# Row sums of 16384 rows: the last store in two halves on two queues, three blocks of rows instead of two, another cut of the last row

## The chip, the cores and the metric

The kernel runs on one core of a Trainium2 chip. The metric is the time of one execution on the device in microseconds (us), as the median of several runs; lower is better. The profile is of one execution, with its times counted from the span's start. SyncE (SP) and ScalarE (ACT) can each issue DMAs; VectorE (DVE) and ScalarE compute here, TensorE and GpSimd do no work of the kernel.

## The reference

```python
x = np.random.randn(32, 512, 1024).astype(np.float32)
return np.sum(x, axis=-1).astype(np.float32)
```

It is 32 x 512 = 16384 rows of 1024 floats (4 KB each), 67.11 MB in all, and one sum for each row: 64 KB of output.

## The kernel before

The 128 partitions take 128 rows each. The rows lie in two blocks. In the first, partition p owns 113 consecutive rows of the input (`BODY`), so neighbouring partitions are 113 x 4 KB = 452 KB apart. In the second, it owns 15 (`LAST`), 60 KB apart. A row sum goes to one column of a result tile: `res_a` with 113 columns, `res_z` with 15. Each tile is stored as one contiguous stretch of the output, 452 B and 60 B a partition.

Loads are all issued by SyncE, in the order of the list `loads` (L86 to L95, issued at L130 to L133): one row into `lead` (the first sum can begin early), then seven groups of 16 rows into the three buffers `xt` in turn, then the last block in pieces. `CUTS = (0, 8, 12, 14)` gives pieces of 8, 4 and 2 rows in one more `xt` buffer; the last row goes into `tail` in two parts, cut at column `CUT = 656`, so 656 and 368 columns. From the fourth group on a load waits until VectorE has finished the group that held its buffer (`freed`, L132). The first two loads are moved into the program's entry (L166 to L175), ahead of the engines' first meeting.

VectorE reduces rows with `tensor_reduce` (`rows_dve`, L58): the lead row, six groups of 16 rows, 9 rows of the seventh. ScalarE takes the other 7 of that group with an activation that accumulates (`rows_act`, L69). Of each of the first two pieces VectorE takes half the rows and ScalarE half, 4 and 4, then 2 and 2. Of the third piece ScalarE takes one row, and VectorE one by `pairs_dve` (L76): it adds the two halves of the row elementwise while it accumulates the sum, so 1024 columns are 512 pairs. The last row is made of two such sums:

```python
pairs_dve(tail, 0, CUT, tail[:, CUT + 14 : CUT + 15], pairs[0])
nc.vector.wait_ge(sems["tail1"], 16)
nc.vector.wait_ge(vec, count["vec"])
pairs_dve(tail, CUT + 14, D + 16, res_z[:, 14:15], pairs[1])
```

The first sums 328 pairs and puts its result beside the columns of the second part, with a zero, so the second sums 185 pairs: the 368 columns, the first result and the zero. VectorE therefore waits at L126 for its own previous result.

SyncE stores twice. The early store of `res_a` (L137) waits for the first part of the last row to land (L134) and for the sums of the groups; the last store of `res_z` (L140) waits for all counts of VectorE (`vec`) and ScalarE (`act`). At the end SyncE waits for the early store, clears the semaphores (L144), and waits for the last store (L145).

Of the kernel before, what the change touches and what calls it, by code (L numbers as in the profile page):

```python
# [6 lines left out]
COPY = mybir.ActivationFunctionType.Copy  # L7
X = mybir.AxisListType.X

LEAD = 1  # L10
G = 16
BODY = LEAD + 7 * G
LAST = 15
BUFS = 3
ACT_ROWS = 7
CUT = 656
CUTS = (0, 8, 12, 14)
EARLY = 2


def row_sums(nc, x: bass.AP, out: bass.AP):
    P = nc.NUM_PARTITIONS
    x_flat = x.flatten_outer_dims()
    R, D = x_flat.shape
    C = R // P
    assert R % P == 0 and C == BODY + LAST
    out_flat = out.rearrange("a (b c) -> (a b c)", c=1)

    def block(r0, n):
        x_b = x_flat[r0 : r0 + P * n].rearrange("(p c) d -> p (c d)", p=P)  # L30
        out_b = out_flat[r0 : r0 + P * n].rearrange("(p c) -> p c", p=P)
        return x_b, out_b

    x_a, out_a = block(0, BODY)
    x_z, out_z = block(P * BODY, LAST)

    def sbuf(name, n):
        return nc.alloc_sbuf_tensor(name, [P, n], F32)

    xt = [sbuf(f"xt{i}", G * D) for i in range(BUFS)]  # L40
    lead = sbuf("lead", LEAD * D)
    tail = sbuf("tail", D + 16)
    pairs = [sbuf(f"pairs{i}", D // 2) for i in range(3)]
    res_a = sbuf("res_a", BODY)
    res_z = sbuf("res_z", LAST)

    names = [f"slot{i}" for i in range(BUFS)] + ["first", "piece0", "piece1", "piece2", "tail0"]
    names += ["tail1", "vec", "act", "early_store", "store"]
    sems = {n: nc.alloc_semaphore(n) for n in names}
    slots = [sems[f"slot{i}"] for i in range(BUFS)]  # L50
    vec, act = sems["vec"], sems["act"]
    numbers = [s.num for s in sems.values()]
    assert numbers == list(range(numbers[0], numbers[0] + len(numbers)))

    count = {"vec": 0, "act": 0}

    def rows_dve(t, j, n, res, c):
        nc.vector.tensor_reduce(  # L58
            out=res[:, c : c + n],
            in_=t[:, j * D : (j + n) * D].rearrange("p (j d) -> p j d", d=D),  # L60
            axis=X,
            op=ADD,
        ).then_inc(vec, 1)
        count["vec"] += 1

    def rows_act(t, j, n, res, c):
        for i in range(n):
            v = t[:, (j + i) * D : (j + i + 1) * D]
            nc.scalar.activation(  # L69
                out=v, in_=v, func=COPY, accum_out=res[:, c + i : c + i + 1]  # L70
            ).then_inc(act, 1)
            count["act"] += 1

    def pairs_dve(t, a, b, acc, pairs):
        h = (a + b) // 2
        nc.vector.tensor_tensor_reduce(  # L76
            out=pairs[:, 0 : h - a], in0=t[:, a:h], in1=t[:, h:b], scale=1.0, scalar=0.0,
            op0=ADD, op1=ADD, accum_out=acc,
        ).then_inc(vec, 1)
        count["vec"] += 1  # L80

    n_bufs = (BODY - LEAD) // G


    freed = {}
    loads = [(0, lead[:, :], x_a[:, 0 : LEAD * D], sems["first"])]  # L86
    for b in range(n_bufs):
        c = LEAD + b * G
        loads.append((b, xt[b % BUFS][:, :], x_a[:, c * D : (c + G) * D], slots[b % BUFS]))
    last = xt[n_bufs % BUFS]  # L90
    for k, (i, j) in enumerate(zip(CUTS, CUTS[1:])):
        loads.append((n_bufs, last[:, i * D : j * D], x_z[:, i * D : j * D], sems[f"piece{k}"]))
    for k, (i, j, gap) in enumerate(((0, CUT, 0), (CUT, D, 16))):
        e = (LAST - 1) * D
        loads.append((0, tail[:, i + gap : j + gap], x_z[:, e + i : e + j], sems[f"tail{k}"]))  # L95


    nc.vector.memset(tail[:, CUT + 15 : CUT + 16], 0.0).then_inc(vec, 1)  # L98
    count["vec"] += 1
    nc.vector.wait_ge(sems["first"], 16)  # L100
    rows_dve(lead, 0, LEAD, res_a, 0)
    for b in range(n_bufs):
        a = ACT_ROWS if b == n_bufs - 1 else 0
        nc.vector.wait_ge(slots[b % BUFS], 16 * (b // BUFS + 1))
        rows_dve(xt[b % BUFS], 0, G - a, res_a, LEAD + b * G)
        freed[b] = count["vec"]
        if a:
            nc.scalar.wait_ge(slots[b % BUFS], 16 * (b // BUFS + 1))
            rows_act(xt[b % BUFS], G - a, a, res_a, LEAD + b * G + G - a)
    body_vec, body_act = count["vec"], count["act"]  # L110

    for k in range(2):
        i, j = CUTS[k], CUTS[k + 1]
        h = (j - i) // 2
        nc.vector.wait_ge(sems[f"piece{k}"], 16)
        rows_dve(last, i, h, res_z, i)
        nc.scalar.wait_ge(sems[f"piece{k}"], 16)
        rows_act(last, i + h, j - i - h, res_z, i + h)
    nc.scalar.wait_ge(sems["piece2"], 16)
    rows_act(last, 13, 1, res_z, 13)  # L120
    nc.vector.wait_ge(sems["piece2"], 16)
    pairs_dve(last, 12 * D, 13 * D, res_z[:, 12:13], pairs[2])
    nc.vector.wait_ge(sems["tail0"], 16)
    pairs_dve(tail, 0, CUT, tail[:, CUT + 14 : CUT + 15], pairs[0])
    nc.vector.wait_ge(sems["tail1"], 16)
    nc.vector.wait_ge(vec, count["vec"])  # L126
    pairs_dve(tail, CUT + 14, D + 16, res_z[:, 14:15], pairs[1])


    for b, dst, src, s in loads:  # L130
        if b >= BUFS:
            nc.sync.wait_ge(vec, freed[b - BUFS])  # L132
        nc.sync.dma_start(out=dst, in_=src).then_inc(s, 16)  # L133
    nc.sync.wait_ge(sems["tail0"], 16)  # L134
    nc.sync.wait_ge(vec, body_vec)
    nc.sync.wait_ge(act, body_act)
    nc.sync.dma_start(out=out_a, in_=res_a[:, :]).then_inc(sems["early_store"], 16)  # L137
    nc.sync.wait_ge(vec, count["vec"])
    nc.sync.wait_ge(act, count["act"])
    nc.sync.dma_start(out=out_z, in_=res_z[:, :]).then_inc(sems["store"], 16)  # L140


    nc.sync.wait_ge(sems["early_store"], 16)
    nc.sync.sem_clear(range(numbers[0], sems["store"].num))  # L144
    nc.sync.wait_ge(sems["store"], 16).then_inc(sems["store"], -16)  # L145


def kernel(tc: tile.TileContext, x: bass.AP, out: bass.AP):
    tc.close()
    tc.compile()  # L150
    nc = tc.nc
    row_sums(nc, x, out)

    sp = mybir.EngineType.SP
    fn = nc.m.functions[0]
    entry, body = None, None
    for blk in fn.blocks:
        ops = [i for i in blk.instructions if i.engine == sp]  # L160
        if entry is None:
            entry = blk
        elif any(i.opcode == "DMACopy" for i in ops):
            body = blk
            break
    code = list(body.instructions)  # L166
    loads = [i for i in code if i.engine == sp and i.opcode == "DMACopy"][:EARLY]
    for load in loads:
        assert not load.sync_info.on_wait
        code.remove(load)  # L170
    body.instructions = code
    code = list(entry.instructions)
    at = next(k for k, i in enumerate(code) if i.engine == sp and i.opcode == "Drain")
    code[at:at] = loads
    entry.instructions = code  # L175
# [29 lines left out]
```

## Time and profile before

| what | value |
|---|---|
| median of 3 runs | 160.99 us (160.79 to 161.18) |
| span of the profiled execution | 159.7 us |
| outside the span, against the median | 1.3 us |
| VectorE busy | 122.6 us (77%) |
| ScalarE busy | 16.3 us (10%) |
| DMA packets | 2160, all on SyncE's queue, 97.8% of the 16 engines' span |

The profile gives the profiled execution's span and no other time of its own; what lies around the span is taken as the difference to the median. Packets are counted with the small ones that report a landing. A stretch of the trace ("windows") gives the busy time of each engine in it, the granted clock, the mean busy share of the 16 DMA engines and GB/s. Short stretches can show a share above 1.00 and uneven GB/s, because a packet is put down to the time at which it is listed.

In the chain of waits, "DMA" stands for the time until a load landed, "SPq" for SyncE issuing a DMA, "DVEq" for VectorE's sequencer. A pair sum shows as two instructions, the sum itself and a read of the accumulator (0.08 us) that overlaps its end.

### The profile page before, as it was taken

Reading aid. Unit: us, or ns where it says so; the run is one execution under the profiler, and the core shown is the slowest. Engines: PE = TensorE matmul, PEld = TensorE weight load, DVE = VectorE, ACT = ScalarE, POOL = GpSimd, SP = SyncE. Lnnn points to the kernel's source line nnn. Section 1 sums busy time; section 2 is a strip of 40 time slices with the busy share of each in tenths; the row PEclk is TensorE's granted clock in tenths of the full one; section 3 lists DMA queues with packets and bytes.
Section 4 is the critical chain, followed back from the end, with each engine's and each line's share of the span. In section 5 each row is a group of like instructions: output and inputs, shape, how many; then the busy total and the mean of one; then the engine's idle time right before and its main releaser. Section 6 shows DMA issues by size and latency. Waiting matters only on the chain.

```text
span 159.7 us, 105 instructions
## 1 busy us (share of the span) xinstructions
DVE 122.6 (77%) x17; ACT 16.3 (10%) x29; POOL 0.2 (0%) x4
## 2 busy tenths in 40 slices
DVE  1100029999499985999779996899949999499984
ACT  3000000000000000000000000000000000196783
POOL 0000000000000000000000000000000000000000
DMA  9969969979799699699699699699796996999993
GB/s 394 525 263 525 509 279 525 460 328 525 328 460 525 263 525 525 263 525 525 263 525 509 279 525 492 295 525 443 345 525 295 492 525 295 476 410 394 435 394 107
DMA packets 2160, 67.18 MB, mean 421 GB/s; under 512 B 496, under 2 KB 624, under 8 KB 880
## 3 DMA queue, kind: packets, MB, share of 16 engines
q1 hardware_dynamic: 2160, 67.18, 97.8%
HBM read 67.11 MB, written 0.07 MB: 421 GB/s over the span
## 4 chain that ended last, share of the span: by engine, by line
DMA 75%; DVE 22%; SPq 1%; issue 0%; DVEq 0%
DMA xt<-in_x_dram 51%; DMA tail<-in_x_dram 24%; DVE res_a L58 22%; SPq L133 1%; DVE pairs L76 1%; DVEq L126 0%; DVE tail L76 0%; DVE res_z L76 0%
## 5 line engine op out<-in xcount | busy, mean ns | idle before, releaser
L58 DVE TENSOR_REDUCE res_a<-xt 128x16 f32<-128x16384 f32 (+1 forms) x7 | 113.1, 16155 | 31.0 <-DMA xt<-in_x_dram 31.0
L69 ACT ACTIVATE xt<-xt 128x1024 f32<-128x1024 f32 x14 | 14.6, 1045 | 139.1 <-DMA xt<-in_x_dram 139.1
L58 DVE TENSOR_REDUCE res_z<-xt 128x4 f32<-128x4096 f32 (+1 forms) x2 | 6.7, 3352 | 0.5 <-DMA xt<-in_x_dram 0.5
L69 ACT ACTIVATION_READ_ACCUMULATOR xt<-xt 128x1 f32 x14 | 2.6, 187 | 0.0
L58 DVE TENSOR_REDUCE res_a<-lead 128x1 f32<-128x1024 f32 x1 | 1.2, 1219 | 1.4 <-DMA lead<-in_x_dram 1.4
L98 DVE MEMSET tail<- 128x1 f32 x1 | 0.1, 59 | 2.0 <-PEq L150 2.0
L69 ACT ACT_TABLE_LOAD x1 | 1.3, 1283 | 1.9 <-PEq L150 1.9
L76 DVE CUSTOM_DVE_ANT_0 pairs<-tail 128x328 f32<-128x328 f32 (+1 forms) x2 | 0.9, 427 | 0.3
L76 DVE CUSTOM_DVE_ANT_0 pairs<-xt 128x512 f32<-128x512 f32 x1 | 0.7, 693 | 0.2 <-DMA xt<-in_x_dram 0.2
L76 DVE DVE_READ_ACCUMULATOR2_ANT res_z<- 128x1 f32 x2 | 0.2, 83 | 0.0
L189 POOL MEMSET const-uint8-127<- 128x1 uint8 x1 | 0.1, 102 | 0.0
L189 POOL MEMSET const-bfloat16-1.0<- 128x1 bf16 x1 | 0.1, 101 | 0.0
L189 POOL MEMSET const-float32-0.0<- 128x1 f32 x1 | 0.1, 98 | 0.2 <-issue 0.2
L189 POOL MEMSET const-float32-1.0<- 128x1 f32 x1 | 0.1, 98 | 0.0
L76 DVE DVE_READ_ACCUMULATOR2_ANT tail<- 128x1 f32 x1 | 0.1, 82 | 0.0
## 6 DMA issues: line engine op xcount, KB each, us to landing
xt<-in_x_dram SPq DMA_DIRECT2D x1, 4096.0 KB, 31.2
xt<-in_x_dram SPq DMA_DIRECT2D x1, 2048.0 KB, 35.7
xt<-in_x_dram SPq DMA_DIRECT2D x1, 1024.0 KB, 37.7
lead<-in_x_dram SPq DMA_DIRECT2D x1, 512.0 KB, 3.4
tail<-in_x_dram SPq DMA_DIRECT2D x1, 328.0 KB, 38.0
tail<-in_x_dram SPq DMA_DIRECT2D x1, 184.0 KB, 37.9
xt<-in_x_dram SPq DMA_DIRECT2D x7, 40.8
out_dram<-res_a SPq DMA_DIRECT2D x1, 56.5 KB, 1.6
```

The source lines that it names most:

```text
L58: nc.vector.tensor_reduce(out=res[:, c : c + n], in_=t[:, j * D : (j + n) * D].rearrange("p (j d) -> p j d", d=D), axis=X, op=ADD,).then_i ...
L69: nc.scalar.activation(out=v, in_=v, func=COPY, accum_out=res[:, c + i : c + i + 1]).then_inc(act, 1)
L76: nc.vector.tensor_tensor_reduce(out=pairs[:, 0 : h - a], in0=t[:, a:h], in1=t[:, h:b], scale=1.0, scalar=0.0, op0=ADD, op1=ADD, accum_out ...
L98: nc.vector.memset(tail[:, CUT + 15 : CUT + 16], 0.0).then_inc(vec, 1)
L133: nc.sync.dma_start(out=dst, in_=src).then_inc(s, 16)
L189: nc = _bacc.Bacc("TRN2", target_bir_lowering=False, num_devices=1)
```

## The change

The 128 rows of a partition are cut into three blocks of 32, 48 and 48 rows, with a result tile for each (`res0` to `res2`), so that all eight groups have 16 rows; neighbouring partitions are 128 KB apart in the first block and 192 KB in the others. The lead row is now the first row of the first group and is loaded into `xt[0]` with a DMA of its own, and the group's other 15 rows by a second. The last group has 16 rows, in pieces of 9, 4 and 2 and a last row cut at column 544 (544 and 480 columns; 272 pairs, then 241). VectorE takes 4 rows of the first piece, as before, and ScalarE 5.

The early store becomes three, of 32, 48 and 32 columns (128, 192 and 128 B a partition), issued one after the other by SyncE once the third piece has landed, not the first part of the last row. The last store has the 16 columns of the last group (64 B a partition, at every 192 B of the output) and is cut by partitions: SyncE issues the store of partitions 0 to 63, ScalarE that of 64 to 127 on its own queue, each after waiting for all counts of `act` and `vec`. SyncE clears the semaphores after the three early stores and ScalarE's half have landed, and waits for its own half last.

```diff
+BLOCKS = (32, 48, 48)
 LEAD = 1
 G = 16
-BODY = LEAD + 7 * G
-LAST = 15
 BUFS = 3
 ACT_ROWS = 7
-CUT = 656
-CUTS = (0, 8, 12, 14)
+CUT = 544
+CUTS = (0, 9, 13, 15)
...
+    for k, n in enumerate(BLOCKS):
+        x_b, out_b = block(r0, n)
+        res = sbuf(f"res{k}", n)
+        for c in range(0, n, G):
+            groups.append((x_b, res, c))
+        stores.append((out_b, res, n))
+        r0 += P * n
+    x_z, res_z, c_z = groups[-1]
...
+    loads = [(0, xt[0][:, 0:D], x_0[:, 0:D], sems["first"])]
+    loads.append((0, xt[0][:, D : G * D], x_0[:, D : G * D], slots[0]))
...
+    def final(queue, p, q, s):
+        dst, src = out_z[p:q, c_z : c_z + G], res_z[p:q, c_z : c_z + G]
+        queue.dma_start(out=dst, in_=src).then_inc(s, 16)
...
+    rows_act(last, G - 2, 1, res_z, c_z + G - 2)
+    nc.scalar.wait_ge(act, count["act"])
+    nc.scalar.wait_ge(vec, count["vec"])
+    final(nc.scalar, P // 2, P, sems["late"])
...
-    nc.sync.wait_ge(sems["tail0"], 16)
+    nc.sync.wait_ge(sems["piece2"], 16)
     nc.sync.wait_ge(vec, body_vec)
     nc.sync.wait_ge(act, body_act)
-    nc.sync.dma_start(out=out_a, in_=res_a[:, :]).then_inc(sems["early_store"], 16)
+    for k, (out_b, res, n) in enumerate(stores):
+        m = n - G if k == len(stores) - 1 else n
+        nc.sync.dma_start(out=out_b[:, 0:m], in_=res[:, 0:m]).then_inc(sems[f"early{k}"], 16)
+    nc.sync.wait_ge(act, count["act"])
     nc.sync.wait_ge(vec, count["vec"])
-    nc.sync.wait_ge(act, count["act"])
-    nc.sync.dma_start(out=out_z, in_=res_z[:, :]).then_inc(sems["store"], 16)
+    final(nc.sync, 0, P // 2, sems["store"])
...
-    nc.sync.wait_ge(sems["early_store"], 16)
+    for k in range(len(stores)):
+        nc.sync.wait_ge(sems[f"early{k}"], 16)
+    nc.sync.wait_ge(sems["late"], 16)
     nc.sync.sem_clear(range(numbers[0], sems["store"].num))
     nc.sync.wait_ge(sems["store"], 16).then_inc(sems["store"], -16)
```

## The prediction

> **What bounds the kernel now.** I read the page first, then the chain of waits, the stretches between block landings, the timeline of the last 4 us, and the issue view.
>
> ```profile
> HBM read 67.11 MB, written 0.07 MB: 421 GB/s over the span
> ...
> DMA 75%; DVE 22%; SPq 1%; issue 0%; DVEq 0%
> ```
>
> The span is 159.7 us, and the loads are nearly all of it. VectorE's 22% of the chain do not make it a second bound, as the stretches between successive landings show (length, busy VectorE, busy ScalarE, POOL, clock, DMA share, GB/s):
>
> ```profile
> 22.76:42.21 19.45, 17.23 (x2) 0.00 (x0) 0.00 (x0) 1.00 1.00 431
> 42.21:61.60 19.39, 17.22 (x1) 0.00 (x0) 0.00 (x0) 1.00 1.00 433
> ...
> 139.04:148.75 9.71, 9.71 (x1) 7.39 (x14) 0.00 (x0) 1.00 0.98 424
> ```
>
> Each 8 MB block takes 19.4 us to land at a DMA share of 1.00, and 17.2 us to reduce. VectorE waits about 2.1 us in each round; a freed buffer is requested while a whole block is still queued. So the time is the load stream, which moves the same 67.11 MB after the change, and then a tail behind its last bytes:
>
> ```profile
> 156.14 1.06 ACT L69 ACTIVATE xt<-xt 128x1024 f32<-128x1024 f32 x1 [0.30 <-DMA xt<-in_x_dram]
> 156.14 0.69 DVE L76 CUSTOM_DVE_ANT_0 pairs<-xt 128x512 f32<-128x512 f32 x1 [0.20 <-DMA xt<-in_x_dram]
> 156.75 0.08 DVE L76 DVE_READ_ACCUMULATOR2_ANT res_z<- 128x1 f32 x1
> 156.96 0.35 SPq L137 DMA_DIRECT2D out_dram<-res_a  x1
> 156.97 0.50 DVE L76 CUSTOM_DVE_ANT_0 pairs<-tail 128x328 f32<-128x328 f32 x1
> ...
> 157.63 0.35 DVE L76 CUSTOM_DVE_ANT_0 pairs<-tail 128x185 f32<-128x185 f32 x1
> 157.91 0.08 DVE L76 DVE_READ_ACCUMULATOR2_ANT res_z<- 128x1 f32 x1
> 158.02 0.34 SPq L140 DMA_DIRECT2D out_dram<-res_z  x1
> ```
>
> Columns are start, duration, engine, line. From 156.97 on VectorE, then the last store, set the end: issued at 158.02, it lands at the end of the span, 1.68 us later. Between the two pair sums lie 0.16 us (157.47 to 157.63): the accumulator read and VectorE's wait for its own count at L126.
>
> **The change, part by part.** Sums are made on this execution: span 159.7, with 1.3 us outside it against the median of 160.99. I keep that 1.3, and so state results as 160.99 plus the change. What a measurement of this kernel can tell from no change is about 0.2%, 0.32 us.
>
> *The cut of the last row (656 to 544 columns).* The two rows of 500 ns (328 pairs) and 354 ns (185 pairs) give 146/143 = 1.02 ns for a pair. 272 pairs then take 0.50 - 0.06 = 0.44 us, and 241 take 0.35 + 0.06 = 0.41. The first part of that row is 112 x 4 x 128 = 57 KB smaller, 0.14 us at 424 GB/s, so it lands near 156.81 instead of 156.95. VectorE is busy with the 512-pair sum until 156.83, and starts at 156.85 instead of 156.97: -0.12. It ends at 157.29; with the same 0.16 the second sum starts at 157.45. The second part lands about 157.4 in either kernel (issued at 119.48, 37.9 us to landing, the end of an unchanged stream), so this cover has only some 0.05 us to spare. Sum: -0.12 - 0.06 + 0.06 = **-0.12**; the last count comes at 157.88 instead of 158.00.
>
> *ScalarE's extra row.* The cuts 9, 13, 15 with one row fewer ahead put the same rows before each landing: pieces land at 148.75, 153.65 and 156.14 as now. ScalarE takes 5 rows of the first piece instead of 4: 1.04 us. It now idles 0.63 ahead of the second piece and 0.30 ahead of the third; that hides 0.93, and its last row ends at most 0.11 later than 157.10 + 0.19 = 157.29. Needed is 157.88: **0**. Without that cover the price would be the 1.04.
>
> *The merged first row, 15 rows in group 0.* Each group lands one row (1.2 us) earlier and is reduced that much earlier; VectorE's 2.1 us of waiting stay. The loads keep their order on SP's queue. **0**, between +0.08 and -0.08 (the difference of one 4 KB row at the stream's rate and the six stretches' spread of 0.07 from their mean).
>
> *Early stores, one becomes three, issued after the third piece (156.14) instead of the first tail part (156.96).* What an issue costs when several follow each other:
>
> ```profile
> 117.58 0.33 SPq L133
> ...
> 117.95 0.44 SPq L133
> ...
> 118.43 0.48 SPq L133
> ...
> 118.96 37.99 DMA tail<-in_x_dram
> ```
>
> Starts 0.37, 0.48 and 0.53 apart. Three from 156.14 end at 157.1 + 0.4 = 157.5, at 0.53 each at 157.7; SP is needed at 157.88. Behind the new wait stand only the stores, no load. Their packets start about 0.83 after an issue, so from 156.97, when the stream's last packets are gone (share 0.01 at 156.90 to 156.95); the third's are over by 158.4, ahead of the last store's. **0**; if a fourth issue queued behind them cost as the third above, +0.14 (0.48 against 0.34).
>
> *The last store, halved.* Its anatomy, in stretches of 0.05 us (after the length: VectorE, ScalarE, POOL, clock, DMA share, GB/s):
>
> ```profile
> 158.80:158.85 0.05, 0.00 (x0) 0.00 (x0) 0.00 (x0) 1.00 0.00 0
> 158.85:158.90 0.05, 0.00 (x0) 0.00 (x0) 0.00 (x0) 1.00 0.41 40
> ...
> 159.00:159.05 0.05, 0.00 (x0) 0.00 (x0) 0.00 (x0) 1.00 0.22 17
> 159.05:159.10 0.05, 0.00 (x0) 0.00 (x0) 0.00 (x0) 1.00 0.03 1
> ```
>
> 0.83 us from issue to the first packet, 0.21 of packets, 0.64 until the landing is seen. The page's two stores compare thus:
>
> ```profile
> out_dram<-res_a SPq DMA_DIRECT2D x1, 56.5 KB, 1.6
> out_dram<-res_z SPq DMA_DIRECT2D x1, 7.5 KB, 1.7
> ```
>
> Seven and a half times the bytes cost no more time. From below, a half saves 0.10 of packets and, if it lands as the 452 B rows do (0.43 from last packet to landing), 0.2 more: -0.30; and half of the 0.49 between the issue's end and the first packet, if that went by rows: -0.25. From above, ScalarE's store is the first of its queue, as the first load was of SP's, with its first packets 1.0 us after the issue, not 0.83: +0.18; and a second issue made behind the first costs 0.37 to 0.53. I take **0**, from the nearest row: the full-width store of 60 B rows, whose time neither bytes nor packets set. The Trainium skill, "DMA: Bandwidth & Descriptors", section "Rules for kernel authors", speaks against the halving: two transfers to disjoint partition halves run over the same 16 DMA engines either way, so one 128-partition transfer is to be used; by it the packets' 0.21 us stay as they are and the sum is -0.05, by the lower end above it would be -0.35. ScalarE's new waits hold back nothing but its own store.
>
> *The close.* SP now waits for the early stores and ScalarE's half before the clear of the semaphores; if both halves land together the clear (0.05) and an instruction start (0.02) come after the landing, where now they lie under the store: **+0.07**.
>
> **Sum:** -0.12 + 0 + 0 + 0 + 0 + 0.07 = -0.05: 160.94, said as 160.9.
>
> **Rivals.**
> *B, the halves land sooner.* -0.12 - 0.30 + 0.07 = -0.35, 160.64, and with the other 0.25 160.39; taken 160.5. For it: 60 B rows have a longer close (0.64) than 452 B rows (0.43), and rows of 64 B, each on its own 64 B, might lose that. Against: issue to landing is 1.6 to 1.7 whatever the size.
> *C, one queue's store is made ready behind the other's.* Both are issued within some 0.05 us. If the second is made ready as a successive issue is, it starts 0.37 to 0.53 late: -0.12 + 0.37 to 0.53 + 0.07 = +0.32 to +0.48; taken 161.4. It decides from 0.37 on. For it: successive issues grow from 0.33 to 0.48, so something behind the queue is shared. Against: those are one queue's.
> *D, the new row pitch slows the stream.* Partitions lie 452 KB apart in the body and 60 KB in the last block now; after, 128 KB (two groups) and 192 KB (six). The two pitches of the trace agree: 9.71 for 8 rows against half of 19.38, 0.2% or 0.3 us on 155; the spread of the six stretches (19.32 to 19.45) is 0.7%, or 1.1 us. 161.3 to 162.1; taken 161.6. It makes the kernel slower from 0.3% on. Against: the stream is level at 433 GB/s for both pitches. The Trainium skill, same page, section "Latency and other measured facts", gives copies 207 GB/s at a pitch of 512 KiB against 214 in full, and far less at 2 MiB; no run here shows such pitches, and were 128 KiB as bad as 512, 3.3% of two groups (38.8 us) would be 1.3 us, 162.2.
> *That the halving does nothing* is in the forecast already.
>
> **Chances.** Forecast 0.42, with its own range 160.68 to 161.3; B 0.24; C 0.19; D 0.15. So faster 0.24, same 0.42, slower 0.34. The range 160.45 to 161.6 leaves out 0.06 of B and 0.08 of D.
>
> **What would show it.** Stretches of 19.4 us between landings: 19.45 and more in the first two is D. The pair sums at 156.85 and 157.45. Three early issues over by 157.7. Both last issues by 157.95, first packets 0.83 later; a gap between the two queues' packets is C. Issue to landing under 1.45 is B. What would make it wrong: a store from ScalarE that starts much later than SP's, or a second tail part that lands after 157.45.

## The result, and the profile after

The changed kernel takes 161.44 us (161.30 to 161.58, 8 runs) against 160.95 (160.68 to 161.19, 8 runs): a ratio of 1.0033, 95% interval 1.0024 to 1.0042. It is slower by a third of a percent, half a microsecond. The forecast was 160.9 and no change.

The stream has not moved. The page, and the stretches between landings (the first one shown is the load of the second group, at the 128 KB pitch; the others are at 192 KB; columns as before):

```profile
HBM read 67.11 MB, written 0.07 MB: 420 GB/s over the span
```

```profile
21.48:40.90 19.42, 16.16 (x2) 0.00 (x0) 0.00 (x0) 1.00 1.00 432
...
99.10:118.45 19.35, 17.22 (x2) 0.00 (x0) 0.00 (x0) 1.00 1.00 434
118.45:137.80 19.35, 17.22 (x1) 0.00 (x0) 0.00 (x0) 1.00 0.95 410
```

The six stretches between these landings take 19.32 to 19.47 us each and 116.32 together, where they took 19.32 to 19.45 and 116.28 before. One of them, the second, is at 19.47 past the 19.45 that the prediction gave as the sign of a slower stream, but the sum of the six shows none. The smaller share and GB/s in the last stretch are not new; before had them in the same place:

```profile
119.69:139.04 19.35, 17.22 (x1) 0.00 (x0) 0.00 (x0) 1.00 0.94 406
```

VectorE and ScalarE begin on the third piece at 156.11 instead of 156.14. The timeline of the changed kernel from there on:

```profile
156.10 1.30 SPq L166 DMA_DIRECT2D out_dram<-res  x3
...
156.78 0.44 DVE L81 CUSTOM_DVE_ANT_0 pairs<-tail 128x272 f32<-128x272 f32 x1
...
157.38 0.41 DVE L81 CUSTOM_DVE_ANT_0 pairs<-tail 128x241 f32<-128x241 f32 x1 [0.15 <-DMA tail<-in_x_dram]
...
157.87 0.53 SPq L137 DMA_DIRECT2D out_dram<-res  x1
157.88 0.54 ACTq L137 DMA_DIRECT2D out_dram<-res  x1
```

Up to the last issue the change is a gain: 157.87 against 158.02. The three early issues are over at 157.40 and in nobody's way. The pause of 0.15 that the second pair sum shows is not new either: from the end of the first sum to the start of the second it is 0.16 us here and was 0.16 before (157.47 to 157.63). The profile puts it down to the load because that came last, at 157.34. But the two issues of the last store take 0.53 and 0.54 us where the one before took 0.34, and their landings are late (issue view: size, us to landing):

```profile
out_dram<-res SPq DMA_DIRECT2D x1, 4.0 KB, 1.7
out_dram<-res ACTq DMA_DIRECT2D x1, 4.0 KB, 2.0
```

The packets show where the time goes, in the same 0.05 us stretches as before (last two columns: DMA share, GB/s):

```profile
159.00:159.05 0.05, 0.00 (x0) 0.00 (x0) 0.00 (x0) 1.00 0.04 5
...
159.20:159.25 0.05, 0.00 (x0) 0.00 (x0) 0.00 (x0) 1.00 0.03 3
159.25:159.30 0.05, 0.00 (x0) 0.00 (x0) 0.00 (x0) 1.00 0.00 0
159.30:159.35 0.05, 0.00 (x0) 0.00 (x0) 0.00 (x0) 1.00 0.32 32
...
159.45:159.50 0.05, 0.00 (x0) 0.00 (x0) 0.00 (x0) 1.00 0.08 7
```

There are two bursts with a gap between them. SyncE's half begins at 159.04, 1.17 us after its issue, where the whole store began 0.83 after. ScalarE's half begins at 159.31, after the other's packets are done: 1.43 after its issue. It lands at 159.85, the clear follows, and the span ends at 160.05.

One number of the starting point needs correcting. The profiled execution of before had a span of 159.7, but the median span of its later runs is 159.5; its last store took 1.68 us to its landing, where the same store took 1.49 in the trace of the kernel with the cut alone, below. So the two traces show only 0.3 of a change that is 0.5 on the medians above.

### The profile page after: what moved, and what is told of

The parts are those of the page before. It is cut to its first block, busy times and chain, and to the rows that moved or that the text cites. A ratio compares the mean times of both kernels' runs of the same rounds, so it can differ in the third digit from the quotient of the medians.

```text
span 160.0 us, 113 instructions
## 1 busy us (share of the span) xinstructions
DVE 121.5 (76%) x17; ACT 17.2 (11%) x31; POOL 0.2 (0%) x4
## 4 chain that ended last, share of the span: by engine, by line
DMA 74%; DVE 22%; SPq 1%; issue 0%
DMA xt<-in_x_dram 50%; DMA tail<-in_x_dram 24%; DVE res L63 22%; SPq L160 1%; DVE pairs L81 0%; DVE res L81 0%
## 5 line engine op out<-in xcount | busy, mean ns | idle before, releaser
L63 DVE TENSOR_REDUCE res<-xt 128x16 f32<-128x16384 f32 (+5 forms) x10 | 119.9, 11994 | 33.9 <-DMA xt<-in_x_dram 33.9
L74 ACT ACTIVATE xt<-xt 128x1024 f32<-128x1024 f32 x15 | 15.6, 1043 | 138.1 <-DMA xt<-in_x_dram 138.1
L81 DVE CUSTOM_DVE_ANT_0 pairs<-tail 128x272 f32<-128x272 f32 (+1 forms) x2 | 0.9, 426 | 0.2 <-DMA tail<-in_x_dram 0.2
```

Of the source, the lines that this page charges most:

```text
L63: nc.vector.tensor_reduce(out=res[:, c : c + n], in_=t[:, j * D : (j + n) * D].rearrange("p (j d) -> p j d", d=D), axis=X, op=ADD,).then_i ...
L74: nc.scalar.activation(out=v, in_=v, func=COPY, accum_out=res[:, c + i : c + i + 1]).then_inc(act, 1)
L81: nc.vector.tensor_tensor_reduce(out=pairs[:, 0 : h - a], in0=t[:, a:h], in1=t[:, h:b], scale=1.0, scalar=0.0, op0=ADD, op1=ADD, accum_out ...
```

## The experiments

My theory at first was that two issues made at the same moment hold each other up. The rivals: the early stores or the 64 B rows slow the last store (1), the new blocks slow the stream (2), ScalarE's queue is slow (3).

**The last store whole again, in the changed kernel.**

```diff
-    nc.scalar.wait_ge(act, count["act"])
-    nc.scalar.wait_ge(vec, count["vec"])
-    final(nc.scalar, P // 2, P, sems["late"])
...
-    final(nc.sync, 0, P // 2, sems["store"])
+    final(nc.sync, 0, P, sems["store"])
...
-    nc.sync.wait_ge(sems["late"], 16)
```

> The changed kernel with its last store whole again: all 128 partitions on SyncE's queue, 64 B a partition, nothing on ScalarE's. Theory (two issues made at once hold each other up): the store goes back to some 1.68 us from issue to the end of the span, against 2.18 in the changed kernel, and the earlier pair sums (issue at 157.87 instead of 158.02) stay: span 159.55, about 160.8 us. Rival 1 (the three early stores just ahead, or the 64 B rows at a 192 B step, slow the last store): it still takes over 2 us, 161.3. Rival 2 (blocks and pitch slow the stream): landings of the pieces later than 156.1, over 161.0 whatever the store takes.

Measured 160.62 us against 160.84, ratio 0.9982 (0.9970 to 0.9994): a little faster than the kernel before, and faster than the changed one. Its timeline, its issue view and the stretches of the packets:

```profile
157.96 0.33 SPq L137 DMA_DIRECT2D out_dram<-res  x1
```

```profile
out_dram<-res SPq DMA_DIRECT2D x1, 8.0 KB, 1.4
```

```profile
158.75:158.80 0.05, 0.00 (x0) 0.00 (x0) 0.00 (x0) 1.00 0.08 9
158.80:158.85 0.05, 0.00 (x0) 0.00 (x0) 0.00 (x0) 1.00 0.70 64
```

Issue 0.33, first packet 0.83 after it, landed after 1.4; from the issue to the end of the span it is 1.44 us, less than the 1.68 that I had expected from before. The same three early stores, the same 64 B rows, the same blocks: rivals 1 and 2 fall, and the whole loss lies in the halving, with the later close that it brings.

**The last store halved, in the kernel before.**

```diff
-    nc.sync.dma_start(out=out_z, in_=res_z[:, :]).then_inc(sems["store"], 16)
+    nc.sync.dma_start(out=out_z[0 : P // 2], in_=res_z[0 : P // 2, :]).then_inc(sems["store"], 16)
+    nc.scalar.wait_ge(act, count["act"])
+    nc.scalar.wait_ge(vec, count["vec"])
+    nc.scalar.dma_start(out=out_z[P // 2 : P], in_=res_z[P // 2 : P, :]).then_inc(sems["late"], 16)
...
+    nc.sync.wait_ge(sems["late"], 16)
```

> The kernel before with this one part of the change: its last store of 60 B rows in halves, partitions 0 to 63 from SyncE, 64 to 127 from ScalarE, and the clear behind both. Theory: issued at 158.02 by both, 2.18 us to the end, span 160.2, about 161.45. Rival 1 (early stores, 64 B rows): neither is here, so the halves cost no more than the 0.07 of the close: 161.0.

161.67 against 160.84, ratio 1.0052 (1.0031 to 1.0072). Issues of 0.53 us on both queues, first packets at 1.17 and 1.39 after them. This one part costs 0.8 us by itself (0.5 to 1.2 by the interval).

**The cut alone, in the kernel before.**

```diff
-CUT = 656
+CUT = 544
```

> The kernel before with this one part of the change: the last row cut at column 544 instead of 656. The changed kernel's trace has the last issue 0.15 us earlier; if that is all the cut's, 160.8 us (ratio 0.999). If the earlier issue comes from elsewhere, no change, 160.95.

160.75 against 160.84, ratio 0.9990 (0.9981 to 0.9999): a gain of about 0.1, at the edge of what these runs resolve. In its profiled execution the second part of the last row lands at 157.54 and the second pair sum starts right after, at 157.59, still with the 0.16 behind the first sum: the cut has all but used up its cover.

**The whole store from ScalarE, in the changed kernel.**

```diff
-    final(nc.scalar, P // 2, P, sems["late"])
+    final(nc.scalar, 0, P, sems["late"])
...
-    final(nc.sync, 0, P // 2, sems["store"])
...
-    nc.sync.wait_ge(sems["store"], 16).then_inc(sems["store"], -16)
```

> The changed kernel with its last store whole and issued by ScalarE alone; SyncE issues none behind the early stores and clears the semaphores after ScalarE's store has landed. Theory (two at once): 1.68 us to the landing as from SyncE, and 0.07 to 0.1 for the clear behind it: 160.9. Rival 3 (a store from ScalarE is slow in itself, or its queue's first use is): the first packet later than 0.84 us after the issue, landing after 1.9 to 2.0 us as in the changed kernel, 161.1 to 161.3.

160.89 against 160.84, ratio 1.0000 (0.9988 to 1.0012). Issue 0.37, first packet 0.87, landing 1.45 after it: a first use of ScalarE's queue costs 0.04. Rival 3 falls.

So far all fits "two at once", but none of these kernels had a half by itself. The next four do, or bear on it.

**One half alone, from SyncE.**

```diff
-    nc.scalar.wait_ge(act, count["act"])
-    nc.scalar.wait_ge(vec, count["vec"])
-    final(nc.scalar, P // 2, P, sems["late"])
...
-    nc.sync.wait_ge(sems["late"], 16)
```

> The changed kernel without ScalarE's half of the last store: the sums of the last 16 columns of partitions 64 to 127 are not stored. It measures the half by itself. Theory (two issues at once): SyncE's issue takes 0.33 to 0.35 us as a whole one's, the first packet 0.84 after it, landing in 1.3 to 1.45. Rival 4 (a store of 64 partitions is slow in itself): issue 0.53, first packet 1.17 after it, landing 1.7, as in the changed kernel.

160.90 in its one run. That is 0.28 over the median of the kernel that stores all of it, but single runs of that one go up to 160.93, so the time alone shows nothing. The timeline and the packets do:

```profile
157.82 0.53 SPq L137 DMA_DIRECT2D out_dram<-res  x1
```

```profile
158.95:159.00 0.05, 0.00 (x0) 0.00 (x0) 0.00 (x0) 1.00 0.05 6
159.00:159.05 0.05, 0.00 (x0) 0.00 (x0) 0.00 (x0) 1.00 0.34 31
```

With nothing beside it the half still takes 0.53 to issue, its first packet comes 1.17 after that, and it lands after 1.70. My theory falls as the main cause: the half is slow in itself (rival 4).

**One half alone, from ScalarE.**

```diff
-    final(nc.sync, 0, P // 2, sems["store"])
...
-    nc.sync.wait_ge(sems["store"], 16).then_inc(sems["store"], -16)
```

> The changed kernel without SyncE's half of the last store: the sums of the last 16 columns of partitions 0 to 63 are not stored; the clear comes after ScalarE's half has landed. Theory: issue 0.37 us and first packet 0.87 after it, as ScalarE's whole store showed, landing 1.3 to 1.45. Rival 4: issue 0.53, first packet 1.43 after it.

161.01 in one run, first packet 1.18 after the issue, landing 1.72:

```profile
157.83 0.52 ACTq L137 DMA_DIRECT2D out_dram<-res  x1
```

So ScalarE's half is no slower than SyncE's; of its 1.43 in the changed kernel, 0.25 come from the other half at the same moment. Each theory explains a part.

**Both halves from SyncE.**

```diff
-    nc.scalar.wait_ge(act, count["act"])
-    nc.scalar.wait_ge(vec, count["vec"])
-    final(nc.scalar, P // 2, P, sems["late"])
...
+    final(nc.sync, P // 2, P, sems["late"])
     final(nc.sync, 0, P // 2, sems["store"])
```

> The changed kernel with both halves issued by SyncE, one after the other, partitions 64 to 127 first. Theory: the first issue is quick (0.34, first packet 0.84 after it), the second comes 0.38 later and takes 0.43 as other successive issues do, and lands about 0.4 after the first: span 159.4 + 0.4 = 159.8, 161.0 us, better than the changed kernel's 161.44. Rival 4 (halves are slow in themselves): two issues of 0.53 and a first packet 1.17 after the second, landing near 160.2, 161.5 or more.

161.65 against 160.87, ratio 1.0054 (1.0037 to 1.0070). Issues of 0.53 and 0.59, the first packet 1.17 after the first, and the second landing at 160.28. It is what rival 4 gave.

**ScalarE's queue used once before.**

```diff
+    nc.scalar.wait_ge(vec, freed[1])
+    nc.scalar.dma_start(out=stores[0][0], in_=stores[0][1][:, :]).then_inc(sems["early0"], 16)
...
-    for k, (out_b, res, n) in enumerate(stores):
+    for k, (out_b, res, n) in list(enumerate(stores))[1:]:
```

> The changed kernel with the first of its three early stores issued by ScalarE at about 60 us, in its idle time, so that its queue has been used once before the end, and only two early stores stand ahead of SyncE's half. Theory (two at once): both last issues still take 0.53, first packets 1.17 and 1.43 after them: no change, 161.4. Rival 3 (first use of the queue) or rival 1 (the third early store): the packets come 0.84 after the issue, 160.9 or less.

161.45 against 160.87, ratio 1.0036 (1.0023 to 1.0049), issues of 0.52 and 0.54, first packets at 1.17 and 1.42: nothing changes. Neither the queue's first use nor the third early store is the cause.

What makes the half slow could be its number of partitions, its bytes, or its few packets. Two kernels tell these apart.

**Halves by columns.**

```diff
-    def final(queue, p, q, s):
-        dst, src = out_z[p:q, c_z : c_z + G], res_z[p:q, c_z : c_z + G]
+    def final(queue, i, j, s):
+        dst, src = out_z[:, c_z + i : c_z + j], res_z[:, c_z + i : c_z + j]
...
-    final(nc.scalar, P // 2, P, sems["late"])
+    final(nc.scalar, G // 2, G, sems["late"])
...
-    final(nc.sync, 0, P // 2, sems["store"])
+    final(nc.sync, 0, G // 2, sems["store"])
```

> The changed kernel with its last store halved by columns, not by partitions: SyncE stores columns 0 to 7 of all 128 partitions, ScalarE columns 8 to 15, 32 B a partition each. Theory as it now stands (a store of 64 partitions is slow in itself, some 0.34 us more until its first packet, and a second one made at the same moment is some 0.27 behind): SyncE's issue 0.35 and first packet 0.84 after it, ScalarE's first packet 0.27 to 0.4 later, the clear behind: span about 0.3 less than the changed kernel's, 161.1. Rival 5 (any second store at the same moment slows both, and 64 partitions are slow only by chance of these runs): issues of 0.53, 161.45.

161.02 against 160.89, ratio 1.0007 (0.9997 to 1.0016). The issue view again:

```profile
out_dram<-res SPq DMA_DIRECT2D x1, 4.0 KB, 1.4
out_dram<-res ACTq DMA_DIRECT2D x1, 4.0 KB, 1.6
```

Issues of 0.33 and 0.38, first packets 0.82 and 0.88 after them. The same bytes in halves are quick when each has 128 partitions, and the second queue's packets are now only 0.08 behind the first's; the 0.27 of the changed kernel belongs to the slow form too. My 0.27 to 0.4 for it was too much. Rival 5 falls.

**A probe of partition counts**, behind the kernel with its last store whole. It rewrites the same sums and loads rows that nobody uses; its total time, 180.1 us in one run, means nothing.

```diff
-    final(nc.sync, 0, P // 2, sems["store"])
+    final(nc.sync, 0, P, sems["store"])
...
+    nc.sync.wait_ge(sems["store"], 16)
+    n = 0
+    for p, q, j in PROBES:
+        dst, src = out_z[p:q, c_z : c_z + j], res_z[p:q, c_z : c_z + j]
+        nc.sync.dma_start(out=dst, in_=src).then_inc(sems["probe"], 16)
+        n += 16
+        nc.sync.wait_ge(sems["probe"], n)
...
```

> The kernel with its last store whole, then stores of the same results made one after the other, each after the one before it has landed: partitions 0-127, 0-63, 64-127, 0-95, 0-79, 0-31, 0-15 of 64 B, 0-127 of 32 B, 0-111 of 64 B; then loads of 128 x 1 KB, 64 x 1 KB, 128 x 512 B into a buffer that is free. It adds some 20 us that mean nothing; what is read is each issue's time and its time to landing. Theory (fewer than 128 partitions cost extra, whatever their bytes): 0.33 to 0.37 and 1.4 for 128 partitions of 64 B or of 32 B, 0.53 and 1.65 to 1.7 for all the others, for the 64-partition load too. Rival 6 (it goes by the bytes or the count of packets): the time changes step by step with the rows, and the 32 B store differs from the 64 B one.

The issue view has the stores by size; at 64 B a partition, 8 KB are 128 partitions, 7 are 112, 6 are 96, 5 are 80, 2 are 32 and 1 is 16. The three of 4 KB are the two of 64 partitions and the one of 128 partitions with 32 B (1.43 by itself):

```profile
out_dram<-res SPq DMA_DIRECT2D x3, 4.0 KB, 1.7
...
out_dram<-res SPq DMA_DIRECT2D x2, 8.0 KB, 1.4
...
out_dram<-res SPq DMA_DIRECT2D x1, 6.0 KB, 1.4
out_dram<-res SPq DMA_DIRECT2D x1, 5.0 KB, 1.4
out_dram<-res SPq DMA_DIRECT2D x1, 2.0 KB, 1.3
...
out_dram<-res SPq DMA_DIRECT2D x1, 7.0 KB, 1.4
```

Not "fewer than 128", as I had expected, and not the bytes: of these counts 64 alone is slow. Its two stores land after 1.72 and 1.66; all other counts lie between 1.31 and 1.43, falling a little with the rows. The load of 64 partitions took 0.52 to issue, with its first packet 1.30 after that; the two of 128 took 0.36, with 0.99 and 0.98.

**The changed kernel cut at partition 80.**

```diff
-    final(nc.scalar, P // 2, P, sems["late"])
+    final(nc.scalar, 80, P, sems["late"])
...
-    final(nc.sync, 0, P // 2, sems["store"])
+    final(nc.sync, 0, 80, sems["store"])
```

> The changed kernel with its last store cut at partition 80 instead of 64: 80 partitions from SyncE, 48 from ScalarE, at the same moment, all else as in the changed kernel. Theory (64 partitions are the slow count, as the probe showed for 64 and not for 32, 80, 96 or 112): both issues 0.33 to 0.38, first packets 0.82 to 0.9 after them, landing 1.4 to 1.6, the clear behind: 161.0 us as the column halves, against 161.44. Rival 5 (two stores by partitions at the same moment are slow whatever the count): issues of 0.53, 161.4.

161.14 against 160.83, ratio 1.0016 (1.0006 to 1.0026); first packets 0.84 and 0.90 after the issues, landings 1.4 and 1.6:

```profile
158.19 0.35 SPq L137 DMA_DIRECT2D out_dram<-res  x1
158.20 0.40 ACTq L137 DMA_DIRECT2D out_dram<-res  x1
```

The ratio is under the changed kernel's 1.0033, though the two intervals just touch (1.0026 and 1.0024), and nearer to the column halves' 1.0007. In this trace the stream ended 0.3 late; free of that is the time from ScalarE's issue to the end of the span, 1.77 us, against 1.78 with the column halves, 2.16 in the changed kernel and, from SyncE's issue, 1.44 with the whole store. Rival 5 falls for parts cut by partitions too.

**A second probe**, with other counts and orders (184.2 us in one run, which again means nothing).

```diff
+PROBES = (
+    (0, 112, 16), (0, 48, 16), (32, 96, 16), (0, 64, 16), (0, 64, 16), (0, 64, 8),
+    (64, 112, 16), (0, 72, 16), (0, 128, 16), (0, 64, 2),
+)
+LOADS = ((0, 64, 256), (0, 80, 256), (0, 64, 256), (0, 48, 256))
```

> A second probe behind the kernel with its last store whole: stores one after the other, each after the last has landed, of partitions 0-111, 0-47, 32-95 (64 of them), 0-63 twice, 0-63 with 32 B, 64-111, 0-71, 0-127, 0-63 with 8 B; then loads of 1 KB rows for 64, 80, 64 and 48 partitions. What is read is each issue's time and the first packet. Theory (it is the count 64): all 64s, at any place, size and position in the sequence, 0.47 to 0.55 and first packet 1.1 to 1.2, loads 1.3; the others 0.31 to 0.36 and 0.8 to 0.85, loads near 1.0. Rival 7 (the first probe's 64s were slow because they came first in their form): the repeated 64 is quick, and 0-47 or 0-111 slow where it comes first.

SyncE's issues in the timeline, in the order of the list from the second on (48, then 64 at partition 32 and 64 at partition 0, later 48 and 72):

```profile
160.85 0.32 SPq L179 DMA_DIRECT2D out_dram<-res  x1
...
162.19 0.63 SPq L179 DMA_DIRECT2D out_dram<-res  x1
...
164.01 0.50 SPq L179 DMA_DIRECT2D out_dram<-res  x1
...
169.07 0.34 SPq L179 DMA_DIRECT2D out_dram<-res  x1
...
170.43 0.36 SPq L179 DMA_DIRECT2D out_dram<-res  x1
```

Every store of 64 partitions is slow, at any place and position, with 64, 32 or 8 B, and also when repeated: issue 0.47 to 0.63, first packet 1.12 to 1.27. The first of them takes longest, more than I had expected (0.63, and its first packet 1.27); the later ones settle at 0.47 and 1.12 to 1.13. All others: 0.32 to 0.36, and 0.79 to 0.85. Loads of 64 partitions issue in 0.49 to 0.52 with a first packet after 1.27 to 1.30, against 0.32 to 0.33 and 0.94 to 0.95 for 48 and 80. Rival 7 falls.

## Why the prediction was wrong

By its own steps:

- *What bounds the kernel*, *the merged first row*, *ScalarE's extra row*, *the early stores at 0*: right. Landings come as before, the early issues end at 157.40 (forecast 157.5 to 157.7), and SyncE is free when it is needed.
- *The cut, -0.12*: right. The sums start at 156.78 and 157.38 (forecast 156.85 and 157.45) and last 0.44 and 0.41 as worked out; the earlier last issue (0.15) has 0.03 from the stream. As the prediction said, the cover is thin: the second part lands at 157.34, 0.04 ahead of the second sum's start, and costs nothing beyond the 0.16 that was there before.
- *The last store, halved, taken at 0 "from the nearest row: the full-width store of 60 B rows"*: this is the step that failed. Against the whole store of 64 B rows the term was +0.55 us, as the sum below shows. The row was near in its bytes a partition, and the prediction showed that bytes do not set the time; it did not have a half's number of partitions, and a store of 64 partitions takes 0.31 (ScalarE) to 0.34 us (SyncE) longer until its first packet, and the second of two such stores at the same moment 0.25 more. A store from ScalarE that starts much later than SyncE's was among the signs of being wrong, and it came (0.27), but SyncE's half was late as well. My upper end, 0.18 for a first use of ScalarE's queue or 0.37 to 0.53 for a successive issue, did not have this among its causes.
- *The close, +0.07*: mis-sized. It cost about 0.17 more than the close of the whole store, because the clear stands wholly behind the later half: from landing to the end 0.20 against 0.03.
- *Rival C* gave 161.4, the time that came, with a second queue made ready 0.37 to 0.53 behind the first. It was 0.27 behind, short of the point from which C was said to decide, and only 0.08 with 128 partitions each. The time fits, the mechanism was a minor part; that the prediction's range, wide because of C and D, holds 161.44 is luck.
- *Rival B*: from the last packet to the landing the whole store of 64 B rows took 0.37, against the 0.64 that the prediction read. But in the trace with the cut alone the same 60 B rows took 0.44, so the 0.64 was mostly of that one execution; a gain from 64 B rows is not shown beyond 0.07, and it needs no halving. *Rival D*: no loss at pitches of 128 and 192 KB.

The Trainium skill, "DMA: Bandwidth & Descriptors", section "Rules for kernel authors", was right that disjoint halves gain nothing: cut at partition 80, where both parts are quick, the ratio is 1.0016, against 0.9982 for the whole store. Halves of 64 partitions cost more again (1.0033).

The sum, between the profiled executions of the changed kernel (160.05) and of the one with the whole store (159.40): last issue (ScalarE's) -0.07, first packet of ScalarE's half 1.43 instead of 0.83, +0.60 (0.04 for ScalarE's queue, 0.31 for 64 partitions, 0.25 for the other half at the same moment), packets and landing -0.05, close +0.17: +0.65, the difference of the spans. The medians of the two kernels, 161.44 and 160.62, differ by 0.8; the rest is the spread of single executions. What the change gained elsewhere, a whole store shows: 0.2%.

Why 64 partitions are slow, and no other count tried, is open: the runs show that the delay comes ahead of the first packet, 0.1 to 0.2 us of it in the issue itself, for stores on both queues and for loads on SyncE's, and nothing of what is done there.

## What to carry to other kernels

The short store at the end cost its latency here, not its bytes (1.4 us for 8 KB, 1.3 for 1 KB): one DMA of all partitions had landed after 1.41 us, when the later part of every cut store still had 0.2 to 0.9 us to go, and a cut over two queues also brought a later close. Before a DMA is cut, time the form it is cut into by itself; here the one count that a half suggests was the slow one of nine. And a price taken from "the nearest row" is only as good as the dimension in which that row is near.

## What the runs showed of the hardware

DMAs of 64 partitions, stores on either queue and loads on SyncE's, took 0.47 to 0.63 us to issue (0.32 to 0.37 for a lone DMA of 16, 32, 48, 72, 80, 96, 112 or 128) and had their first packet some 0.3 to 0.4 us later than the others; two stores at the same moment on two queues ran one behind the other, 0.27 to 0.28 us apart, where two of 128 partitions were 0.08 apart. Whole last stores with rows of 64 B landed 1.40 to 1.45 us after the issue in every trace; with rows of 60 B it was 1.49 in one and 1.68 in another.
